# A hybrid three-branch layer on one core: one gate job fewer ahead of branch B, more gate work beside its units, and other block orders in branch A and in the output

## The chip, the cores and the metric

The kernel runs on one core of one Trainium2 chip. The metric is the device time of one launch in microseconds (us). A mark such as L648 is line 648 of the kernel before. The engines are PE (TensorE, matmuls and transposes), DVE (VectorE), ACT (ScalarE), POOL (GpSimd) and SP (SyncE, which here only issues DMAs; all loads and stores of this kernel go through its one queue, in order).

## What is computed

One layer on 2048 tokens of width 1024, in float32. After a layer norm, one wide projection (7592 columns) feeds three token mixers and their gates; in the reference's own words, cut:

```python
def _dsa_attention(q, k, v, iq, ik, iw):        # branch A, 8 heads, one key head
    ...
        _, idx = lax.top_k(score, n_sel)        # 256 keys of each query
    ...
        p = jax.nn.softmax(logits, axis=-1).astype(v.dtype)
        return jnp.einsum('bqhk,bqkd->bqhd', p, v_sel)

def _diff_attention(q, k, v, lam):              # branch B, 4 heads
    ...
        p = jax.nn.softmax(logits, axis=-1)
        a = (p[:, :, 0] - lam * p[:, :, 1]).astype(v.dtype)
        return jnp.einsum('bhqs,bshe->bqhe', a, v)

def _memory_attention(q, mk, mv):               # branch C, 4 heads, 256 memory tokens
    ...
```

Attention in A and B is chunk-causal: the block of queries number b (128 tokens, b = 0 to 15) sees (b + 1) * 128 keys, so block 15 is sixteen times as long as block 0. Each branch's output is multiplied by a SiLU gate ("sg"), projected to 1024 columns, weighted by a sigmoid gate ("tm"), summed, projected once more, added to the input and normalised.

## The kernel before, in words

Every float32 operand of a matmul is held as a high and a low part; `mm3` (L76 to L79) makes one product of three matmuls (high by high, high by low, low by high).

**Stages.** (1) The projections for A and B and A's top-k, whose result is a table of biases per block (`bias_d`, stored at L595). (2) The *gate jobs*: the list JOBS has 20 of them (2 "cq", 6 "sg", 12 "tm"), each for 256 columns and one half of the tokens. `gate_steps` does one job: a 2 MB load of weights `w` (L232), then 32 steps, each an `mm3` of 128x512 into PSUM tile `dps`; after each 8 steps a quarter of the job is finished by ACT and DVE and stored from tile `do` (L329, 256 KB, "sg_d" or "tm_d"). (3) Branch B. (4) Branch A. (5) Projections of B and C ("yps"), which need branch B and the gates only. (6) The projection of A for four pairs of blocks (`stage1`, tile `gT`), then per pair the last projection (tile `fz`) and the norm.

**Gate jobs of the first half of the tokens** are dealt out in three shares by `GB`: GB[0] jobs run as a block before branch B, the next GB[1] are handed out step by step within branch B, and the rest run after `run(fill)` (L915 to L918) together with the setup of the memory tokens (`do<-in_mem_dram`, L414, transposed by PE into `psT`, L183). The rest is written behind branch A, but the Tile framework's scheduler sets the order there and mixes it with branch A.

**Branch B** is a list of 64 units (4 heads, in each the blocks 15 down to 0). Inside `manual_schedule` the order of PE's instructions is that of the code. A unit has logits (tiles `lg` and `lgx`, L648 and L649, from keys `kg` and queries `bq`), a softmax on DVE and ACT, a mixture of two softmaxes on DVE (`mix`, L742, tile `P`), transposes (`pt`, L761) and products with the values (`ops`, L753). Logits run up to two units ahead. Between the parts, `pump(us)` hands out gate steps, counted at 0.69 us each:

```python
    for g in range(3, -1, -1):
        load_k(0, g)
        load_v(0, g)
    ...
    with tc.manual_schedule(engines={PE.engine}):
        pump(10.0)
        for _ in units[0].logits():
            pump(1.0)
    ...
            share = FILL[0] + FILL[1] * (u.b + 1)
    ...
                pump(share / m)
```

The loads of head 0 (`load_k` L679, `load_v` L685) and of the queries (`load_q`, L695) stand in SP's queue behind the last store of the top-k table, and SP issues in order. Keys and values of the next head are loaded as the tiles of the old one come free (after blocks 12, 8, 4 and 0). The output of a unit is stored at L791 (`ob_d`).

**Branch A** is `attn_a(b)`, called for b = 15 down to 0 (L912). Before the first block, keys `KA` (L848, 1 MB) and values `VA` (L850) are loaded into space that branch B leaves; each block loads its queries by eight DMAs (`aq`, L861) and its biases (L865). Per pair of heads there are logits with a running minimum on DVE, exponentials on ACT, transposes (`apt`), a split on ACT and DVE, and products (`aops`).

**Output order.** `PORD` is the order of the pairs of blocks in stage 6, and `LAST` the block whose final projection is cut into four pieces instead of two.

Of the kernel before, what the change touches and what calls it, by code (L numbers as in the profile page):

```python
# [22 lines left out]
NB = S // 128  # L23
NP = NB // 2
# [11 lines left out]
GV = 3  # L36
AHEAD = 1
EARLY = 4
PORD = list(range(NP - 1, -1, -1))
LAST = 2 * PORD[-1] + 1  # L40
WO = (1, 1)
YT = 8
YO = 1
APR = 2
GB = (4, 12)
FILL = (3.2, 0.08)
SQ_SCALE = 2.0 ** -80
SQ_LIM = 3.4028234663852886e38 * SQ_SCALE

# [9 lines left out]
def tile_layer(ctx, tc, x, mem, ln_in_g, ln_in_b, w_in, w_mem_kv, diff_lambda, diff_norm_g,  # L59
# [88 lines left out]
    def pool(name, bufs, space=None, side="left"):  # L148
        kw = {} if space is None else {"space": space}
        return tc.alloc_tile_pool(name=name, bufs=bufs, side=side, reuse_waits="tile", **kw)  # L150
# [59 lines left out]
    def reload(p):  # L210
        SP.dma_start(pair_of(p), ht_d[p])
# [182 lines left out]
    def gates(half, jobs, between=()):  # L394
        between = list(between)
        for i, (kind, c0, idx) in enumerate(jobs):
            yield from gate_steps(kind, half, c0, idx)
            if between:
                between.pop(0)()
        for f in between:  # L400
            f()

    def run(steps):
        for _ in steps:
            pass
# [11 lines left out]
    def dense_mem(j):  # L417
        w = dw.tile([128, 2, KT, 256], F32R, name="w")
        for i in range(2):
            for k in (4 * i, 4 * i + 2):  # L420
                raw = dw.tile([128, 2, 256], F32, name="wr", bufs=2)
                SP.dma_start(raw, w_view(w_mem_kv, k * 128, 2, 256 * j, 256))
                split(w[:, 0, k:k + 2], w[:, 1, k:k + 2], raw, G, G)
        ps = dqs.tile([128, 2, 256], F32, name="dps")
        for i in range(2):
            c = slice(i * 128, (i + 1) * 128)
            if j < 2:
                for k in range(KT):
                    mm3(ps[:, i], w[:, 0, k, c], w[:, 1, k, c], hm[0][:, 0, k], hm[0][:, 1, k], k == 0, k == KT - 1)
            else:  # L430
                for k in range(KT):
                    mm3(ps[:, i], hm[0][:, 0, k, c], hm[0][:, 1, k, c], w[:, 0, k], w[:, 1, k], k == 0, k == KT - 1)
        for i in range(2):
            o = dw.tile([128, 2, 256], F32R, name="do", bufs=3)
            if j < 2:
                split(o[:, 0], o[:, 1], ps[:, i], A, V)
                SP.dma_start(mk_d[:, 2 * j + i], o.bitcast(F32))
            else:
                h0 = 2 * (j - 2)
                ov = o.rearrange("p a (h d) -> p (a h d)", d=128).rearrange("p (h a d) -> p h a d", h=2, a=2)  # L440
                pv = ps[:, i].rearrange("p (h d) -> p h d", d=128)
                split(ov[:, :, 0], ov[:, :, 1], pv, A, V)
                SP.dma_start(mv_d[:, i, h0:h0 + 2].rearrange("p h a d -> p (h a d)"),
                             o.bitcast(F32).rearrange("p a c -> p (a c)"))
# [349 lines left out]
    for p in range(4):  # L794
        with tc.high_priority():
            reload(p)
    run(gates(0, JOBS[:GB[0]]))
    fill = gates(0, JOBS[GB[0]:GB[0] + GB[1]])
    owed = [0.0]

    def pump(us):
        owed[0] += us
        while owed[0] > 0:
            t = next(fill, None)
            if t is None:
                return
            owed[0] -= t
# [5 lines left out]
    with tc.manual_schedule(engines={PE.engine}):  # L813
        pump(10.0)
        for _ in units[0].logits():
            pump(1.0)
        units[0].mix()
        ahead = 1
        for i, u in enumerate(units):
            new = []  # L820
            while ahead < len(units) and ahead <= i + 2 and sum(x.slots for x in units[i:ahead + 1]) <= PB:
                new.append(units[ahead])
                ahead += 1
            share = FILL[0] + FILL[1] * (u.b + 1)
            m = 2 * (u.b // 4 + 1)
            n = sum(2 * (x.b // 4 + 1) for x in new)
            lg = (None for x in new for _ in x.logits())
            j = 0
            nxt = units[i + 1] if i + 1 < len(units) else None
            for t, _ in enumerate(u.values()):  # L830
                pump(share / m)
                while (j + 1) * m <= (t + 1) * n:
                    next(lg)
                    j += 1
                if t == m // 2 and nxt is not None and nxt not in new:
                    nxt.mix()
            for _ in lg:
                pass
            u.store()
            if nxt in new:  # L840
                nxt.mix()
# [67 lines left out]
            V.tensor_tensor(oo, oo, rc[:, 4 * h4:4 * h4 + 4, None].to_broadcast([128, 4, 64]), op=ALU.mult)  # L909
        SP.dma_start(oa_d[b], o.rearrange("p h d -> p (h d)"))  # L910

    for b in range(NB - 1, -1, -1):  # L912
        attn_a(b)

    run(fill)  # L915
    mp = pool("mp", 1)
    run(gates(0, JOBS[GB[0] + GB[1]:], [mem_setup] + [(lambda j=j: dense_mem(j)) for j in range(4)]))
    mp.release()  # L918
# [139 lines left out]
    def accs(ap, bufs):  # L1058
        return [ap.tile([128, 2, 256], F32, name="facc", bufs=bufs) for _ in range(4)]

    wo = []
    for i in range(EARLY):
        p = PORD[i]
        acc = accs(fs, 3)
# [20 lines left out]
    def ready(i):  # L1085
        if i >= NP:
            return
        p = PORD[i]
        acc = accs(fp, 4)
        if i < EARLY:  # L1090
            for u in range(4):
                SP.dma_start(acc[u], mg_d[p][:, 2 * u:2 * u + 2])
        else:
            stage1(p, acc)
        MT[p] = fp.tile([128, 2, KT, 256], F32R, name="fmT", bufs=AHEAD + 1)
        for u in range(4):
            H, L = (MT[p][:, a, 2 * u:2 * u + 2] for a in range(2))
            A.activation(H, acc[u], AF.Copy, scale=0.5)
            V.scalar_tensor_tensor(L, acc[u], 0.5, H.bitcast(F32), op0=ALU.mult, op1=ALU.subtract)

    def stage2(b):
        hh = fp.tile([128, D], F32, name="fh", bufs=3)
        SP.dma_start(hh, h_d[b])
        mT = MT[b // 2][:, :, :, 128 * (b % 2):128 * (b % 2) + 128]
        nz = 4 if b == LAST else 2
        for n in range(nz):
            c = slice(n * (D // nz), (n + 1) * (D // nz))
            z = fq.tile([128, 512], F32, name="fz")[:, :D // nz]
            for k in range(KT):
                mm3(z, mT[:, 0, k], mT[:, 1, k], wo[k][:, 0, c], wo[k][:, 1, c], k == 0, k == KT - 1)  # L1110
            V.scalar_tensor_tensor(hh[:, c], hh[:, c], ALPHA, z, op0=ALU.mult, op1=ALU.add)
        mu, rs = norm_stats(fp, hh, nz)
        if b != LAST:
            V.tensor_scalar(hh, hh, mu, rs, op0=ALU.subtract, op1=ALU.mult)
            G.tensor_tensor(hh, hh, gln, op=ALU.mult)
            V.tensor_tensor(hh, hh, bln, op=ALU.add)
            SP.dma_start(out[b * 128:(b + 1) * 128, :], hh)
            return
        for c in (slice(0, 512), slice(512, 1024)):
            V.scalar_tensor_tensor(hh[:, c], hh[:, c], mu, gln[:, c], op0=ALU.subtract, op1=ALU.mult)  # L1120
            V.scalar_tensor_tensor(hh[:, c], hh[:, c], rs, bln[:, c], op0=ALU.mult, op1=ALU.add)
            SP.dma_start(out[b * 128:(b + 1) * 128, c], hh[:, c])
# [3 lines left out]
    for p in range(NP):  # L1126
        ready(p + AHEAD)
        stage2(2 * PORD[p])
        stage2(2 * PORD[p] + 1)
    fq.release()  # L1130
# [54 lines left out]
```

## Time and profile before

| | us |
|---|---|
| three runs | 2928.38, 2924.34, 2923.38 |
| median | 2924.34 |
| profiled execution | 2925.13 |
| its span, first to last instruction | 2923.3 |
| PE busy in the span | 2778.1 (95%) |
| DVE, ACT, POOL busy | 2053.1, 1401.7, 864.6 |
| mean granted clock of PE | 0.982 |

The profiled execution has 1.8 us around its span. "Busy" is the time in which an engine has an instruction running; the clock is given as a share of 2.4 GHz, so that 0.50 is 1.2 GHz. The share of DMA is the mean busy share of the core's 16 DMA engines.

### The profile page before, as it was taken

To read this page: it belongs to the slowest core of one execution; us is meant where nothing else is said; L and a number is where in the kernel's file an instruction comes from. 1 tells how busy PE (TensorE), PEld (TensorE's weight loads), DVE (VectorE), ACT (ScalarE), POOL (GpSimd) and SP (SyncE) were. 2 spreads that over 40 slices of the span, in tenths; PEclk is the share of its full clock that TensorE was granted. 3 is DMA by queue.
4 is the path that set the end of the run, shared out by engine and by line. 5 is a ranking of instruction groups with operands and counts; after the bars stand their busy time and mean duration, and the time that the engine had idled before them with its cause. 6 is when DMAs were issued, how large, how long until landed. Compare 5 with 4: busy or idle time off the path is not lost.

```text
span 2923.3 us, 49093 instructions
## 1 busy us (share of the span) xinstructions
PE 2778.1 (95%) x17488; PEld 2490.2 (85%) x17488; DVE 2053.1 (70%) x4885; ACT 1401.7 (48%) x2716; POOL 864.6 (30%) x1270
## 2 busy tenths in 40 slices
PE   6899999999999989999999998998999999988998
PEld 6799989987788877788888887887999899987887
DVE  7179978898657887677777773447777777775554
ACT  3256755774346870344444442446555655552010
POOL 7454333235433302022222323121222222211322
PEclk9999999999999999999999999999999999998999
DMA  9666555564554576434334335235333333358542
GB/s 359 233 210 237 202 179 172 169 231 171 201 173 167 190 268 203 148 114 142 109 120 131 119 99 160 97 118 170 104 104 99 118 113 111 117 170 268 198 155 73
DMA packets 332020, 476.35 MB, mean 163 GB/s; under 512 B 28928, under 2 KB 252544, under 8 KB 323584
## 3 DMA queue, kind: packets, MB, share of 16 engines
q1 hardware_dynamic: 331776, 473.23, 49.5%
q8 instruction: 138, 2.26, 0.3%
q14 instruction: 106, 0.87, 0.1%
HBM read 271.25 MB, written 201.88 MB: 162 GB/s over the span
## 4 chain that ended last, share of the span: by engine, by line
PE 68%; DMA 7%; DVE 6%; issue 3%; POOL 2%; ACT 2%; SPq 1%; POOLq 0%; DVEq 0%; ACTq 0%
PE dps L77 9%; PE dps L78 9%; PE dps L79 9%; PE ops L753 4%; PE aops L898 4%; PE apt L893 3%; PE lg L648 3%; PE lg L649 3%; PE yps L77 2%; PE yps L78 2%; PE yps L79 2%; PE pt L761 2%; PE fz L77 2%; PE fz L78 2%; PE fz L79 2%
## 5 line engine op out<-in xcount | busy, mean ns | idle before, releaser
L77 PE MATMUL dps<-H,w 128*128 128x512 f32 x1280 | 518.5, 405 | 20.0 <-DVE do L328 5.7
L78 PE MATMUL dps<-H,w 128*128 128x512 f32 x1280 | 505.6, 395 | 0.0
L79 PE MATMUL dps<-H,w 128*128 128x512 f32 x1280 | 504.2, 394 | 0.0
L77 PE MATMUL dps<-w,H 128*128 128x256 f32 (+1 forms) x1152 | 342.1, 298 | 15.4 <-ACT w L71 8.6
L79 PE MATMUL dps<-w,H 128*128 128x256 f32 (+1 forms) x1152 | 339.8, 296 | 2.3 <-DVE H L74 2.3
L78 PE MATMUL dps<-w,H 128*128 128x256 f32 (+1 forms) x1152 | 340.7, 296 | 0.8 <-POOL w L74 0.8
L556 ACT ACTIVATE ja<-sall,thr 128x1280 bf16<-128x1280 f32 (+4 forms) x224 | 301.9, 1348 | 74.7 <-DVE thr L552 69.1
L543 DVE TENSOR_SCALAR_CACHE_REDUCE jd<-sall,thr 128x1408 bf16<-128x1408 f32 (+6 forms) x231 | 330.8, 1432 | 6.3
L77 PEld LDWEIGHTS dps<-H,w 128*128 128x128 f32 x1280 | 243.8, 190 | 64.8 <-issue 9.7
L79 PEld LDWEIGHTS dps<-H,w 128*128 128x128 f32 x1280 | 243.1, 190 | 51.2
L78 PEld LDWEIGHTS dps<-H,w 128*128 128x128 f32 x1280 | 243.8, 190 | 38.2
L651 DVE CUSTOM_DVE_ANT_0 AP<-lg,bias 128x512 f32<-128x512 f32 (+3 forms) x304 | 181.8, 619 | 124.7 <-PE lg L649 61.5
L516 DVE SCALAR_TENSOR_TENSOR sall<-ir,iw,sall 128x512 f32<-128x512 f32 (+3 forms) x266 | 191.9, 768 | 70.6 <-ACT ir L512 68.1
L77 PEld LDWEIGHTS dps<-w,H 128*128 128x128 f32 x1152 | 223.5, 194 | 18.1 <-ACT w L71 9.3
L71 ACT CAST apr<-apt 128x512 fp32r<-128x512 f32 (+1 forms) x288 | 157.5, 562 | 160.7 <-PE apt L893 129.5
L79 PEld LDWEIGHTS dps<-w,H 128*128 128x128 f32 x1152 | 223.1, 194 | 3.5 <-DVE H L74 2.7
L78 PEld LDWEIGHTS dps<-w,H 128*128 128x128 f32 x1152 | 223.5, 194 | 3.0 <-POOL w L74 2.2
L74 DVE TENSOR_TENSOR apr<-apt,apr 128x512 fp32r<-128x512 f32 (+1 forms) x288 | 185.5, 656 | 57.1 <-ACT apr L71 55.4
L898 PE MATMUL aops<-apr,VA 128*128 128x256 f32 x1088 | 209.0, 299 | 14.9 <-ACT apr L71 6.5
L69 POOL TENSOR_SCALAR w<-wr 128x512 fp32r<-128x512 f32 x120 | 87.1, 734 | 424.7 <-PE dps L79 339.2
L885 ACT ACTIVATE AP<-AP,anm 128x1024 f32<-128x1024 f32 (+7 forms) x192 | 172.1, 900 | 67.7 <-DVE anm L882 64.1
L512 ACT ACTIVATE ir<-ips 128x512 f32<-128x512 f32 (+3 forms) x304 | 150.0, 550 | 105.4 <-PE ips L507 92.0
(250 smaller groups left out, 6835.9 us busy)
## 6 DMA issues: line engine op xcount, KB each, us to landing
w_d<-w SPq DMA_DIRECT2D x28, 2048.0 KB, 7.3
w<-w_d SPq DMA_DIRECT2D x28, 2048.0 KB, 8.8
wr<-in_w_in_dram SPq DMA_DIRECT2D x108, 256.0 KB, 3.3
tm_d<-do SPq DMA_DIRECT2D x96, 256.0 KB, 2.9
bq<-qb_d SPq DMA_DIRECT2D x128, 128.0 KB, 3.3
aq<-qa_d SPq DMA_DIRECT2D x128, 128.0 KB, 3.1
yt<-tm_d SPq DMA_DIRECT2D x64, 256.0 KB, 3.5
sg_d<-do SPq DMA_DIRECT2D x48, 256.0 KB, 2.6
```

The costliest lines, as they stand in the source:

```text
L71: A.copy(H, src)
L74: el.tensor_tensor(L, src, H.bitcast(F32), op=ALU.subtract)
L77: PE.matmul(ps, lH, rH, start=start, stop=False)
L78: PE.matmul(ps, lH, rL, start=False, stop=False)
L79: PE.matmul(ps, lL, rH, start=False, stop=stop)
L512: A.activation(r[:, :cn], ps[:, :cn], AF.Relu)
L516: V.scalar_tensor_tensor(s[:, c0:c0 + cn], r[:, :cn], iw[:, h:h + 1], s[:, c0:c0 + cn], op0=ALU.mult, op1=ALU.add)
L543: V.tensor_scalar(jd[:, :L], sc[b], t.bitcast(F32)[:, i:i + 1], None, op0=op, op1=ALU.add, accum_out=dst[:, i:i + 1])
L556: A.activation(ja[:, :L], sc[b], AF.Sign, bias=thr.bitcast(F32)[:, i:i + 1], scale=-1.0, accum_out=cnt[:, i:i + 1])
L651: V.tensor_tensor_reduce(P[:, c0:c0 + cn], ps[:, :cn], bias[:, c0:c0 + cn], scale=-0.125, scalar=-LOW, op0=ALU.add, op1=ALU.min, accum_out ...
L885: A.activation(p[:, c0:c1], p[:, c0:c1], AF.Exp, bias=nm[:, e:e + 1], scale=-1.0, accum_out=sm[:, hd, i:i + 1])
L898: PE.matmul(o_ps.rearrange("p a d -> p (a d)"), VA[:, k0 + i], pr[:, a, i].rearrange("p e q -> p (e q)"), start=(k0 + i == 0 and a == 0), ...
```

## The change

Five edits, none of which changes what is computed or how many matmuls there are (17488 in both). The order of the output pairs becomes 0 to 7, and with it the block in four pieces becomes 15. One gate job fewer runs before branch B, and one more is handed out within it. The share of a unit goes from 3.2 + 0.08 (b + 1) to 3.7 + 0.065 (b + 1) us, and each chunk of the first logits is followed by 2.0 instead of 1.0 us of gate steps. Branch A's blocks run in another order.

```diff
-PORD = list(range(NP - 1, -1, -1))
+PORD = list(range(NP))
 LAST = 2 * PORD[-1] + 1
...
-GB = (4, 12)
-FILL = (3.2, 0.08)
+GB = (3, 13)
+FILL = (3.7, 0.065)
...
         pump(10.0)
         for _ in units[0].logits():
-            pump(1.0)
+            pump(2.0)
...
-    for b in range(NB - 1, -1, -1):
+    for b in [7, 0, 6, 1, 5, 2, 4, 3, 8, 9, 10, 11, 12, 13, 14, 15]:
         attn_a(b)
```

What this does to the order, at three places. The first is SP's queue at the end of the top-k and the start of branch B (`bias_d_128` is the last table of biases, `kg`, `vg`, `bq` are head 0's keys, values and queries, `sg_d` a finished quarter of a gate job). Before:

```order
L595 DMA bias_d_128<-pf 128x2048
L679 DMA kg<-kb_d_3_148 64x2x512 x2
L329 DMA sg_d_0_179<-do 128x512
L685 DMA vg<-vb_d_6_159 128x512
L685 DMA vg<-vb_d_7_160 128x512
...
L695 DMA bq<-qb_d_7_136 64x2x256 x2
L329 DMA sg_d_1_180<-do 128x512
L695 DMA bq<-qb_d_7_136 64x2x256 x2
```

Now:

```order
L595 DMA bias_d_128<-pf 128x2048
L679 DMA kg<-kb_d_3_148 64x2x512 x2
L685 DMA vg<-vb_d_6_159 128x512
L685 DMA vg<-vb_d_7_160 128x512
...
L695 DMA bq<-qb_d_7_136 64x2x256 x4
L695 DMA bq<-qb_d_6_135 64x2x256 x4
L329 DMA sg_d_0_179<-do 128x512
```

Up to the first pair of `kg` the queue is the same row for row (430 rows); then three stores of gate quarters that stood among the sixteen key and value loads and the first queries stand behind them. On PE, the first `lg` of branch B is row 6459 before and row 6363 now: 96 matmuls `dps` (32 steps) that stood ahead of it are gone from there, and nothing else ahead of it has moved. Behind it, 69 `dps` matmuls instead of 36 stand among the first unit's logits, 9 instead of 6 of them after its last.

The second place is SP's queue where the keys of head 3 begin to be loaded (`w` is the next gate job's 2 MB). Before:

```order
L791 DMA ob_d_219<-o 128x128
L329 DMA tm_d_1_196<-do 128x512
L791 DMA ob_d_218<-o 128x128
L679 DMA kg<-kb_d_0_149 64x2x512 x2
L695 DMA bq<-qb_d_6_143 64x2x256
...
L232 DMA w<-w_d_10527 128x4096
```

Now:

```order
L791 DMA ob_d_219<-o 128x128
L695 DMA bq<-qb_d_7_144 64x2x256
L791 DMA ob_d_218<-o 128x128
L232 DMA w<-w_d_10527 128x4096
L329 DMA tm_d_1_196<-do 128x512
L679 DMA kg<-kb_d_0_149 64x2x512 x2
```

The 2 MB load has moved from behind the keys to just ahead of them. The same meeting at the start of head 2 has `w` a few DMAs ahead of `kg` before and directly ahead of it now, and at the start of head 1 `w` has moved from ahead of `kg` to behind it.

The third is PE at the end of branch B and the start of branch A, from the last `ops` on (`psT` are transposes of the memory tokens). Before, 72 matmuls `dps` stand between the last `ops` and these rows:

```order
L648 MATMUL lg<-KA_19071,aq 128x512 x2
L649 MATMUL lg<-KA_19071,aq 128x512 x2
L183 MATMUL psT<-idf,do 128x128 x4
L648 MATMUL lg<-KA_19071,aq 128x512
L649 MATMUL lg<-KA_19071,aq 128x512
```

Now 14 matmuls `dps` stand between the last `ops` and these:

```order
L183 MATMUL psT<-idf,do 128x128 x12
L648 MATMUL lg<-KA_19071,aq 128x512 x2
L649 MATMUL lg<-KA_19071,aq 128x512 x2
L183 MATMUL psT<-idf,do 128x128 x4
L77 MATMUL dps<-H_257,w 128x512
```

58 matmuls have left the stretch in which PE waits for `KA` and the first `aq`, and three loads of memory tokens (`do`) and one of their weights now stand in SP's queue near the last `ob_d` store, ahead of `KA`. In all, 1216 instead of 1095 `dps` matmuls stand between branch B's first `pt` and its last `ops`. Further down, among the loads of the weights of stage 5, eight `aq` loads and one store of branch A now stand in SP's queue where there were none.

## Rows read from the trace of the kernel before

**Rows 1.** The page's busy times: engine, us, share, instructions.

```profile
PE 2778.1 (95%) x17488; PEld 2490.2 (85%) x17488; DVE 2053.1 (70%) x4885; ACT 1401.7 (48%) x2716; POOL 864.6 (30%) x1270
```

**Rows 2.** Windows from B's head to the end; columns in the first row.

```profile
core 0: us, PE busy (x) PEld busy (x) DVE busy (x) ACT busy (x) POOL busy (x), PEclk, DMA share, GB/s
1157.76:1181.10 23.34, 21.93 (x98) 17.86 (x96) 2.75 (x4) 2.39 (x4) 0.00 (x0) 1.00 1.03 278
1181.10:1201.06 19.96, 15.15 (x53) 11.79 (x53) 8.99 (x28) 5.39 (x6) 0.00 (x0) 0.83 0.46 163
1201.06:1788.26 587.20, 576.40 (x3350) 498.71 (x3350) 435.19 (x1521) 274.79 (x520) 159.69 (x441) 0.99 0.36 116
1788.26:1808.08 19.82, 16.74 (x76) 13.60 (x74) 0.59 (x3) 2.54 (x5) 5.41 (x11) 1.00 0.94 295
1808.08:1819.20 11.12, 6.55 (x28) 4.62 (x28) 4.59 (x14) 2.42 (x5) 3.68 (x5) 0.69 0.76 245
1819.20:1974.20 155.00, 153.17 (x934) 135.15 (x932) 70.28 (x182) 65.45 (x125) 23.22 (x25) 1.00 0.31 107
1974.20:2001.80 27.60, 20.70 (x118) 17.13 (x119) 23.77 (x51) 19.95 (x39) 1.36 (x2) 0.81 1.05 336
2001.80:2593.30 591.50, 574.11 (x4447) 542.85 (x4445) 439.31 (x1222) 346.12 (x813) 141.32 (x142) 1.00 0.36 107
2593.30:2629.40 36.10, 28.86 (x203) 26.56 (x203) 22.91 (x83) 15.05 (x48) 3.83 (x3) 0.91 0.69 215
2629.40:2668.50 39.10, 30.19 (x207) 28.61 (x207) 17.80 (x26) 9.40 (x16) 5.35 (x4) 0.83 0.93 306
2668.50:2923.30 254.80, 244.37 (x1338) 209.13 (x1336) 141.38 (x213) 28.93 (x48) 65.69 (x57) 0.99 0.47 153
```

**Rows 3.** A window in the gate jobs, PE alone; columns as above.

```profile
1139.62:1150.73 11.11, 11.11 (x50) 1.00 0.56 180
```

**Rows 4.** Timeline of PE at B's head: start, us, instruction, [idle before, releaser].

```profile
1157.76 0.39 PE L77 MATMUL dps<-H,w 128*128 128x512 f32 x1
...
1181.10 0.47 PE L648 MATMUL lg<-kg,bq 128*128 128x512 f32 x1 [1.41 <-DMA bq<-qb_d]
...
1182.68 0.77 PE L649 MATMUL lg<-kg,bq 128*128 128x512 f32 x1 [1.11 <-DMA bq<-qb_d]
...
1201.06 0.63 PE L761 MATMUL pt<-idf,P 128*128 128x128 f32 x4 [3.70 <-DVE P L742]
```

**Rows 5.** Timeline of SP's queue at B's head: start, us of issue, DMA.

```profile
1157.56 0.32 SPq L595 DMA_DIRECT2D bias_d<-pf  x1
1157.93 1.76 SPq L679 DMA_DIRECT2D kg<-kb_d  x2
1159.99 0.34 SPq L329 DMA_DIRECT2D sg_d<-do  x1
...
1174.83 0.33 SPq L329 DMA_DIRECT2D sg_d<-do  x1
1175.92 5.58 SPq L695 DMA_DIRECT2D bq<-qb_d  x6
```

**Rows 6.** Timeline of PE inside branch B: its waits at new heads.

```profile
1338.69 0.55 PE L648 MATMUL lgx<-kg,bq 128*128 128x512 f32 x1 [1.75 <-DMA kg<-kb_d]
...
1488.15 0.47 PE L648 MATMUL lg<-kg,bq 128*128 128x512 f32 x1 [3.17 <-DMA kg<-kb_d]
...
1503.21 0.47 PE L648 MATMUL lg<-kg,bq 128*128 128x512 f32 x1 [1.19 <-DVE mx L658]
...
1635.89 0.47 PE L648 MATMUL lg<-kg,bq 128*128 128x512 f32 x1 [1.92 <-DMA kg<-kb_d]
```

**Rows 7.** DMA issues: transfer, number, KB each, median us to landing.

```profile
w<-w_d SPq DMA_DIRECT2D x28, 2048.0 KB, 8.8
...
aq<-qa_d SPq DMA_DIRECT2D x128, 128.0 KB, 3.1
```

**Rows 8.** Timeline of SP's queue at the start of branch A.

```profile
1792.91 0.32 SPq L791 DMA_DIRECT2D ob_d<-o  x1
...
1795.21 0.42 SPq L848 DMA_DIRECT2D KA<-ka_d  x1
...
1796.14 5.08 SPq L861 DMA_DIRECT2D aq<-qa_d  x5
```

## The prediction

> **What bounds the kernel now.** I read the busy times first. PE is busy for 95% of the span [rows 1], no other engine for more than 70%, and the change leaves the number of matmuls as it is. So the time can only move by what PE loses: idle time, and time at a low granted clock. Second, I cut the span from branch B on into windows at the places where PE's work changes, and took as the loss of each its idle time plus (1 - clock) times its length [rows 2]. That gives, in order: B's head 1.4 and 8.2 us (windows 1 and 2), the body of B 16.7, the passage from B to A 3.1 and 8.0, A beside the last gate jobs 1.8, the passage to "yps" 12.1, yps beside A 17.4, the end of A 10.5, up to the first "fz" 15.6, the rest 13. Nothing ahead of 1157.76 us changes its order. Third, I looked in the timelines at what ends the waits inside these windows, and in the order at what now stands there.
>
> The sum is made against the profiled execution (2925.13 us, 0.8 above the median of 2924.34); the sum of differences is then added to the median.
>
> **B's head.** In the gate jobs PE does 49 steps of 128x512 from 1139.62 to 1150.73, 0.227 us each [rows 3]. The 96 matmuls that no longer stand ahead of the first logits are 21.8 us of work. It was exactly the work that covered the loads: the store of the last table of biases is issued at 1157.56, the first keys at 1157.93 [rows 5], and PE's first logits wait for the queries until 1181.10 and, for their second half, until 1182.68 [rows 4]. The table comes from DVE at the end of the top-k, which the change does not touch, and SP's queue holds keys, values and queries behind it. So PE will arrive at its first logits at 1157.76, where now the first of the 96 starts, and stand still until the queries land.
>
> When is that? Keys, values and the four query loads of the first unit are 4.72 MB (16 of 256 KB, 4 of 128 KB), the table is 0.52 MB. In the window in question the DMA engines are full (share 1.03) and move 278 GB/s [rows 2]. Three gate stores of 256 KB, the first and last of which are in [rows 5], no longer stand among them: 0.79 MB, 2.8 us at that rate. The second half of the first logits thus starts at 1182.68 - 2.8 = 1179.9, and PE is idle for 22.1 us where it was for 2.5 (1.41 + 1.11). The wait for the mixture on DVE, 3.70 us [rows 4], shrinks by the three matmuls that now stand behind the last logits, 0.7 us. Sum: 22.1 - 2.5 - 0.7 = **+18.9**. From below, I take the densest stretch of the trace, 336 GB/s [rows 2]: 5.24 MB need 15.6 us, which leaves 15.6 - 2.5 - 0.7 = +12.4. From above, without any gain from the stores: 24.9 - 2.5 = +22.4. I stay near the upper part because the 278 GB/s are of these very transfers, and the 336 are of others.
>
> The Trainium skill speaks against so long a wait: "DMA: Bandwidth & Descriptors", section "Specifications", gives about 358 GB/s as what one core gets from HBM, by which 5.24 MB would take 14.6 us and this term would be +11.4. The trace does not agree here: it shows full engines at 278 GB/s. The rule has its place among the rivals.
>
> What happens to the 21.8 us? They are not lost: the steps are now handed out within B, so that they leave the end of the program shorter, but only if they fall into holes of PE, or push other work into holes. Otherwise PE's work is the same, and the idle time is added in full.
>
> **The body of B.** 121 more matmuls stand between first pt and last ops, 27.4 us at 0.227. They make units longer and so help against waits on DVE: three waits for "mx" of 1.19 us each (one of them stands in [rows 6]). What else is idle there is the wait for the keys of a new head, 1.75, 3.17 and 1.92 us; with 3.6 for mx that is 10.4 of the 10.8 idle us of the window [rows 2, 6]. Unit times don't touch the landing of the keys as such: they are loaded when a tile of the old head comes free. But the weights of a gate job, 2 MB that take 8.8 us [rows 7], have moved against them in the queue: at the first new head to behind the keys (-1.75), at the second to directly ahead, at the third from behind to ahead. Each of the latter two costs between 0 and 8.8 us; I take half, 4.4 each, since logits run two units ahead. Waits for mx and the low clock behind a wait give back about 3. Sum: -1.75 + 8.8 - 3 = **+4**, with -16.7 (the whole loss of the window) and +12 as the ends.
>
> **From B to A.** The outputs of the last unit are stored 4.65 us after the last ops (1788.26 to 1792.91), KA is issued 2.3 us later and the first logits of A come 12.87 us after that (1795.21 to 1808.08) [rows 2, 8]. The distance is set by transfers and stays at about 19 us, but of PE's 72 gate matmuls in it 14 are left (3.2 us), and 12 short transposes (1.3 us). The handed-out work has run out too early: 4 x (16 x 3.7 + 0.065 x 136) + 10 + 16 = 298 us are asked for, 13 jobs of 32 steps at 0.69 are 287. Idle time there is about 15 instead of 3.1 us; of the work taken away 17 matmuls (3.9 us) now stand in the stretch behind, which lost 8.0. Sum: 11.8 - 3.8 = **+8**, from +2 (the tm_d store ahead of KA goes faster, and the stretch behind fills) to +13.
>
> **A beside the last gate jobs.** Short blocks have more waits per matmul than block 15, but gate work lies beside them: **+1** (0 to +3).
>
> **The passage to yps.** Here the engines are full with the weights of B's and C's projections (share 1.05 at 336 GB/s [rows 2]), and eight aq loads and a 256 KB store of A now stand among them: 1.3 MB, 3.9 us: **+4** (0 to +8).
>
> **yps beside A.** Blocks 8 to 15 now run here and at the end, in which DVE and ACT have long pieces of work; the loss of 17.4 should fall a little: **-4** (-12 to +6).
>
> **The end of A.** Before, the last blocks are the shortest, with hardly any matmuls to hide a softmax, and 10.5 us are lost. Now block 15 is last, with long runs of transposes and products: **-9** (-10.5 to -4).
>
> **Up to the first fz.** The stage waits for weights and gate tiles whatever the pair's number: **-2** (-5 to +3). The output order itself is free: all pairs cost the same, and the last block is cut in four either way. 0.
>
> Sum: 18.9 + 4 + 8 + 1 + 4 - 4 - 9 - 2 = +20.9, so 2925.13 becomes 2946.0 and the median 2924.34 becomes **2945 us**.
>
> **The rivals.** A measurement of this kernel tells 0.2% (5.8 us) from no change.
>
> *The holes in B close.* If the added gate work covers all of B's waits, the body gives back 16.7 instead of costing 4: 20.9 - 20.7 = +0.2, 2924.5 us, no change. For it: the holes are waits of 1 to 3 us, and a unit gets 0.3 to 0.5 us more gate work. Against: three of them wait for keys that SP issues late, and two got a 2 MB load ahead. 0.14.
>
> *The end closes* (the other side). What is lost from 2001.80 to 2668.50 is 17.4 + 10.5 + 15.6 = 43.5 us. If long blocks at the end of A run beside the loads and products of stage 5 and 6 so that nothing is lost there, the first terms (+31.9) and the passage (+4) stand against -43.5: -7.6, 2917 us. It decides from 36 us given back on, and counts as faster from 42. For it: no short block is left where gate work is gone. Against: 15.6 of it wait for loads after A. 0.08.
>
> *The loads are quicker alone.* At 336 GB/s the head costs 12.4 instead of 18.9: 2938.5 us. Against it, the full engines at 278. 0.08. By the 358 GB/s of the Trainium skill ("DMA: Bandwidth & Descriptors", section "Specifications") the estimate would be 2937.5 us.
>
> *SP's queue jams under short blocks.* Each block issues eight aq loads, five in 5.08 us [rows 8], so 8.1 us per block. Blocks 0 and 1 have less work than that; two blocks waited out in full add 16 us: 2961 us. Against it: gate jobs lie beside them. 0.10.
>
> **How the numbers follow.** The forecast has 0.60. The terms' ends, taken as independent (the root of the sum of squares), reach 25 us below and 17 above 2945, of which I take nine tenths below, so the range is 2922 to 2963. It takes in the first rival and the last two. Faster by over 0.2% is the second alone, 0.08; within 0.2% the first, 0.14; slower the rest, 0.78.
>
> **What would show it.** In the changed profile PE stands idle from 1157.8 to about 1180 with the queries' DMA as releaser, and DMA share near 1. The waits of 3.17 and 1.92 for kg grow, that of 1.75 goes. Between last ops and first lg of A some 15 us are idle. No wait for amx of several us is left at A's end. The forecast is wrong in kind if PE does not wait 20 us at B's head, or if the stretch from 2001.80 on gives back more than 30 us.

## The result and the profile after

The changed kernel takes 2952.05 us (median of four runs, 2949.79 to 2956.82), the kernel before beside it 2925.2: the ratio is 1.0108, with a 95% interval of 1.0088 to 1.0128. It is slower, by 27 us (the medians). The profiled execution took 2949.79 us, with a span of 2948.0, against 2925.13 and 2923.3. The mean granted clock is 0.978 instead of 0.982, PE is busy for 2775.9 us.

The same windows as in [rows 2], cut at the same events, on the changed kernel (window, us, busy time of each engine with its count, PEclk, DMA share, GB/s; the seventh and eighth end at the first "yps" and the last):

```profile
1160.70:1178.34 17.64, 0.17 (x1) 0.03 (x1) 0.00 (x0) 0.00 (x0) 0.00 (x0) 0.64 1.05 278
1178.34:1203.16 24.82, 21.60 (x86) 17.08 (x86) 9.69 (x29) 5.99 (x7) 0.00 (x0) 0.91 0.41 136
1203.16:1826.60 623.44, 605.18 (x3472) 522.91 (x3472) 442.27 (x1524) 278.50 (x526) 160.81 (x441) 0.98 0.36 115
1826.60:1843.19 16.59, 5.66 (x29) 4.22 (x28) 2.67 (x6) 2.51 (x5) 7.93 (x13) 0.74 0.78 247
1843.19:1855.11 11.92, 9.23 (x29) 6.65 (x30) 3.11 (x9) 1.71 (x3) 1.89 (x2) 0.65 0.60 153
1855.11:1981.72 126.61, 126.61 (x781) 113.23 (x780) 50.63 (x166) 49.29 (x108) 22.69 (x24) 1.00 0.38 125
1981.72:2024.07 42.35, 31.30 (x176) 24.88 (x174) 33.83 (x107) 28.40 (x67) 1.45 (x2) 0.88 1.02 302
2024.07:2620.27 596.20, 584.44 (x4507) 552.43 (x4506) 456.66 (x1234) 356.21 (x825) 141.22 (x142) 1.00 0.35 105
2620.27:2651.32 31.05, 27.70 (x225) 26.46 (x224) 18.11 (x32) 11.73 (x21) 3.81 (x3) 1.00 0.58 171
2651.32:2690.91 39.59, 28.84 (x211) 26.98 (x210) 16.51 (x26) 8.56 (x15) 5.20 (x4) 0.87 0.89 304
2690.91:2948.00 257.09, 243.20 (x1335) 209.27 (x1333) 140.81 (x214) 29.68 (x49) 62.32 (x57) 0.99 0.47 152
```

The first row is the new hole: PE is idle for 17.5 us at branch B's head, with full DMA engines (share 1.05) at 278 GB/s, where [rows 2] have 21.93 us of work. In the timeline of PE (start, us, instruction, idle before and releaser), against [rows 4]:

```profile
1160.48 0.39 PE L79 MATMUL dps<-H,w 128*128 128x512 f32 x1
1178.34 0.77 PE L648 MATMUL lg<-kg,bq 128*128 128x512 f32 x1 [17.47 <-DMA bq<-qb_d]
1179.39 0.77 PE L649 MATMUL lg<-kg,bq 128*128 128x512 f32 x1 [0.28 <-DMA bq<-qb_d]
1179.95 0.63 PE L77 MATMUL dps<-H,w 128*128 128x512 f32 x1
```

PE comes to its first logits 2.9 us later than 1157.76, though the order ahead of it is the same; the queries land at the time that the prediction gave, to 0.5 us, but by two errors that cancel: the loads were issued 1.3 us later and took 1.8 us less than it had said. SP's queue there, against [rows 5], has no gate store between the loads and the queries any more:

```profile
1158.88 0.32 SPq L595 DMA_DIRECT2D bias_d<-pf  x1
1159.25 1.36 SPq L679 DMA_DIRECT2D kg<-kb_d  x2
...
1170.85 7.07 SPq L695 DMA_DIRECT2D bq<-qb_d  x8
1182.82 0.33 SPq L329 DMA_DIRECT2D sg_d<-do  x1
```

Inside branch B, the waits for the keys of new heads, against [rows 6]:

```profile
1346.33 0.47 PE L648 MATMUL lgx<-kg,bq 128*128 128x512 f32 x1 [1.07 <-DMA kg<-kb_d]
...
1504.35 0.76 PE L648 MATMUL lg<-kg,bq 128*128 128x512 f32 x1 [7.50 <-DMA kg<-kb_d]
...
1662.21 0.77 PE L648 MATMUL lg<-kg,bq 128*128 128x512 f32 x1 [4.20 <-DMA kg<-kb_d]
```

1.75, 3.17 and 1.92 us have become 1.07, 7.50 and 4.20. At the second of them SP's queue shows the 2 MB of a gate job just ahead of the keys:

```profile
1493.06 0.32 SPq L232 DMA_DIRECT2D w<-w_d  x1
1493.47 0.58 SPq L679 DMA_DIRECT2D kg<-kb_d  x1
1494.15 0.57 SPq L329 DMA_DIRECT2D tm_d<-do  x1
1494.77 0.58 SPq L679 DMA_DIRECT2D kg<-kb_d  x1
```

Inside branch B the waits for "mx", the minima that DVE takes of a unit's logits, which were 3.6 us before, are still there:

```profile
PE lg L648 <- DVE mx L658: 3.0, 2, 1.9
PE lgx L648 <- DVE mx L658: 1.8, 1, 1.8
```

(Instruction, who was waited for: us in total, times, longest.)

**Where the 24.7 us went.** The table below takes for each stretch its time less its matmuls at their pace (0.227 us for 512 columns, 0.12 for 256; the counts are those of the order), and shows the difference to the kernel before, in the profiled executions. The stretches end at B's first "pt", B's last "ops", A's first "apt", the last "dps", the first "yps", the last "yps", the first "fz", the last "fz". The columns e1 to e12 are the experiments further down. In five kernels whose order is the same up to A (before, e3, e5, e11, e12) the first row differs by up to 7 us and the second by 3, so smaller differences say nothing. Each column is a single execution: that of e8 is 7 us faster than e8's median, that of e12 5 us.

| us against before | after | e1 | e2 | e3 | e4 | e5 | e6 | e7 | e8 | e9 | e10 | e11 | e12 |
|---|---|---|---|---|---|---|---|---|---|---|---|---|---|
| up to B's first pt | +16.3 | +16.8 | +0.4 | +1.6 | +6.7 | -1.6 | -1.3 | +17.2 | -4.2 | -2.4 | -6.2 | -3.8 | -5.7 |
| body of B | +8.6 | +4.2 | +18.0 | -0.6 | +8.9 | -3.2 | +20.8 | -1.3 | -3.3 | +6.6 | -1.2 | -1.0 | -1.3 |
| B to A | +7.9 | -10.7 | -0.7 | -2.7 | +7.7 | -1.9 | -0.7 | -10.7 | -10.7 | +9.0 | -1.8 | +0.2 | -5.5 |
| A beside gate jobs | -2.2 | +0.4 | -2.7 | -0.3 | -2.2 | -1.0 | -3.5 | +2.6 | +0.6 | +0.9 | -0.7 | 0.0 | +12.4 |
| up to yps | +6.7 | +1.1 | +9.0 | +6.1 | +10.6 | +8.2 | +2.6 | +2.9 | +4.0 | +9.0 | +8.6 | -0.1 | +4.6 |
| yps beside A | -7.2 | -9.6 | -13.6 | -7.2 | -7.1 | -6.4 | -3.0 | +6.9 | -2.9 | +0.4 | -6.1 | -0.7 | -0.6 |
| up to the first fz | -7.9 | -3.5 | -2.0 | +13.4 | -5.6 | -13.0 | +3.4 | +3.1 | -6.4 | -12.0 | -12.1 | +18.5 | -4.8 |
| fz | +2.5 | -1.9 | -6.9 | +0.1 | -1.4 | -0.6 | -6.6 | +1.0 | +0.2 | -0.2 | +0.7 | -0.2 | -0.5 |

### The profile page after: what moved, and what is told of

It is laid out like the page before. It is cut to its first block, busy times and chain, and to the rows that moved or that the text cites. A ratio compares the mean times of both kernels' runs of the same rounds, so it can differ in the third digit from the quotient of the medians.

```text
span 2948.0 us, 49101 instructions
## 1 busy us (share of the span) xinstructions
PE 2775.9 (94%) x17488; PEld 2489.7 (84%) x17488; DVE 2059.1 (70%) x4885; ACT 1401.7 (48%) x2716; POOL 859.8 (29%) x1270
## 4 chain that ended last, share of the span: by engine, by line
PE 67%; DMA 8%; DVE 6%; issue 3%; ACT 2%; POOL 2%; SPq 0%; POOLq 0%; DVEq 0%; ACTq 0%
PE dps L77 10%; PE dps L78 10%; PE dps L79 10%; PE ops L753 4%; PE aops L898 3%; PE lg L648 3%; PE lg L649 3%; PE apt L893 3%; PE pt L761 2%; PE yps L77 2%; PE yps L78 2%; PE yps L79 2%; PE fz L79 2%; PE fz L78 2%; PE fz L77 2%
## 5 line engine op out<-in xcount | busy, mean ns | idle before, releaser
L77 PE MATMUL dps<-H,w 128*128 128x512 f32 x1280 | 520.7, 407 | 18.9 <-DVE do L328 5.9
```

Source lines behind the costliest of these rows:

```text
L77: PE.matmul(ps, lH, rH, start=start, stop=False)
```

## The experiments

All were timed beside the kernel before, on one chip per group of four; the medians of before were 2920.7, 2922.5 and 2922.0 us. Theory: the loss is the sum of what the stretches lose, above all B's head, where 96 matmuls no longer cover the loads. Rivals: branch A's order carries the loss; or the moved work fills other holes.

**e1: one gate job fewer ahead of B, alone.**

```diff
-GB = (4, 12)
+GB = (3, 13)
```

> The kernel before with one edit alone: GB = (3, 13). Theory (the loads of branch B's head need the 96 matmuls ahead of the first logits as cover): 13 to 17 us slower than before at the head, PE idle there 15 to 18 us, and since only one of the jobs moves, nothing of it comes back; in all 2938 to 2945 us. Rival 1 (the loss lies in branch A's block order and its loads): within 4 us of before. Rival 2 (the 96 matmuls come back as filling of other holes): within 4 us of before, although the idle time at the head is there.

2918.68 us, ratio 1.0000 (0.9990 to 1.0011): no change. The total is what rival 2 said, and the theory's is wrong. But the hole is there, 18.77 us, with full DMA engines at 292 GB/s (the first line is the window up to the first logits, the second is of PE's timeline):

```profile
1158.47:1177.39 18.92, 0.15 (x1) 0.03 (x1) 0.00 (x0) 0.00 (x0) 0.00 (x0) 0.61 1.05 292
1177.39 0.77 PE L648 MATMUL lg<-kg,bq 128*128 128x512 f32 x1 [18.77 <-DMA bq<-qb_d]
```

It comes back further on. The old FILL asks for 266 us in branch B, and thirteen jobs give 287, so that some 21 us of gate steps are left at B's end. They fill the passage to A entirely, which lost 11 us before. The two windows from the last "ops" to A's first "apt", against the fourth and fifth window of [rows 2]:

```profile
1782.19:1802.96 20.77, 20.77 (x94) 17.21 (x93) 0.59 (x3) 2.54 (x5) 2.89 (x8) 1.00 0.99 311
1802.96:1816.80 13.84, 13.84 (x63) 11.40 (x61) 4.14 (x13) 3.46 (x6) 0.00 (x0) 1.00 0.62 226
```

Busy for every one of 34.6 us, at full clock. A further 9.6 us less are lost beside A, under the same block order; why was not settled.

**e2: the change with the old GB.**

```diff
-GB = (3, 13)
+GB = (4, 12)
```

> The changed kernel with GB put back to (4, 12). Theory: the head is as before (PE idle under 4 us), 13 to 17 us come back; the gate steps handed out in branch B run out earlier (298 us asked, 265 there), so the passage from B to A stays as costly as in the change: 2932 to 2940 us. Rival 1 (branch A's order): 2945 or more. Rival 2: as the change, 2950, since the holes in B are no longer filled.

2927.01 us, 1.0022 (1.0011 to 1.0033): 25 us less than the change, more than expected. The head's hole is gone (waits of 1.29 and 1.25 us); but the body of B costs 18 us, and the gain beside and after A is larger than in the change. The passage to A, which was expected to cost as much as in the change, costs no more than before (-0.7).

**e3: branch A's order alone.**

```diff
-    for b in range(NB - 1, -1, -1):
+    for b in [7, 0, 6, 1, 5, 2, 4, 3, 8, 9, 10, 11, 12, 13, 14, 15]:
```

> The kernel before with branch A's new block order alone. Theory: the passage to the projections of B and C costs 4 to 8 us more, the stretch beside A and A's end give back 10 to 15: 2916 to 2926 us. Rival 1 (the loss of the change lies in this order): 2935 or more.

2934.26 us, 1.0050 (1.0033 to 1.0066): slower, against the theory. The stretch up to the first "fz" loses 13 us more. PE's waits there (engine, instruction, who was waited for: us in total, times, longest):

```profile
PE gT L77 <- ACT yoT L945: 12.0, 3, 6.9
PE gT L942 <- DMA fo<-oa_d: 5.9, 1, 5.9
```

Before, in the same stretch:

```profile
PE lg L648 <- DVE amx L658: 4.5, 1, 4.5
PE gT L77 <- ACT yoT L945: 1.8, 2, 1.5
PE gT L942 <- DMA fo<-oa_d: 0.3, 1, 0.3
```

The old output order begins with pair 7, blocks 15 and 14, which this order of A computes last. Stage 6 now waits for A's last outputs: in SP's queue its loads stand directly behind A's last store.

```profile
2614.97 0.32 SPq L910 DMA_DIRECT2D oa_d<-ao  x1
2616.99 0.80 SPq L1049 DMA_DIRECT2D fo<-oa_d  x2
```

**e4: queries first at B's head, in the change.**

```diff
+    load_q(0, NP - 1)
     for g in range(3, -1, -1):
         load_k(0, g)
+    for g in range(3, -1, -1):
         load_v(0, g)
```

> The changed kernel with one edit: at branch B's head the four query loads of the first unit are issued first, then the four key tiles, then the values (0.5 + 2.1 MB instead of 4.7 MB have to land for the first unit's logits). Theory: PE's idle time at the head falls from 17.5 to between 4 and 9 us, and the time by 8 to 12, to 2940 to 2944 us. Rival 2 (the idle time at the head is not on the path, or is only moved to the wait for the mixture): less than 3 us gained.

2943.58 us, 1.0081 (1.0063 to 1.0099): 8.5 us less than the change by the medians, 8 by the ratios, whose intervals just overlap. PE stands for 7.84 us instead of 17.47:

```profile
1169.47 0.77 PE L648 MATMUL lg<-kg,bq 128*128 128x512 f32 x1 [7.84 <-DMA kg<-kb_d]
```

The rest of the program loses what it lost in the change, within the noise of the table. The hole at the head is on the path there.

**e5: both orders, without the edits in branch B.**

```diff
-PORD = list(range(NP - 1, -1, -1))
+PORD = list(range(NP))
...
-    for b in range(NB - 1, -1, -1):
+    for b in [7, 0, 6, 1, 5, 2, 4, 3, 8, 9, 10, 11, 12, 13, 14, 15]:
```

> The kernel before with branch A's new order and the new output order, nothing else. Theory: the new output order begins with pairs that branch A finished long ago, so the wait for A's last outputs that the block order alone brought (13 us up to the first fz) turns into the 8 us gain that the change showed there: 2908 to 2920 us. Rival (branch A's order costs 10 us by itself): 2930 or more.

2906.96 us, 0.9954 (0.9937 to 0.9970): faster by 13 us (the ratio), at the far end of what was expected. Up to the first "fz" 13 us less are lost, instead of 13 more in e3; the 4.5 us wait for "amx" at A's end, shown under e3 for the kernel before, is not there any more. The two lines of e3 here:

```profile
PE gT L77 <- ACT yoT L945: 5.5, 2, 4.7
PE gT L942 <- DMA fo<-oa_d: 2.2, 2, 2.0
```

**e6: the new FILL and the 2.0 us alone.**

```diff
-FILL = (3.2, 0.08)
+FILL = (3.7, 0.065)
...
-            pump(1.0)
+            pump(2.0)
```

> The kernel before with the new FILL and the 2.0 us beside the first logits, nothing else. Theory (handing out more than there is costs in branch B, because the steps cover nothing in the early units and are missing in the last): B's body loses 14 to 20 us more than before, the passage to A about the same as before: 2930 to 2942 us. Rival (the new FILL is harmless; the head and branch A carry the loss): 2916 to 2926.

2936.56 us, 1.0055 (1.0037 to 1.0073): slower, as expected. B's body loses 20.8 us more. Among its waits the keys grow to 11.9 us from 5.1, and new ones appear at L779, in the last units, where the steps have run out (no gate matmul stands in B's last 19 us, 1805.7 to 1824.9):

```profile
PE lg L648 <- DMA kg<-kb_d: 11.9, 2, 7.6
PE ops L753 <- DVE o L779: 8.1, 3, 4.4
```

**e7: the change with the old FILL and 1.0 us.**

```diff
-FILL = (3.7, 0.065)
+FILL = (3.2, 0.08)
...
-            pump(2.0)
+            pump(1.0)
```

> The changed kernel with the old FILL and the old 1.0 us beside the first logits. Theory: PE is still idle 18 us at B's head, but the job moved into branch B is not used up there, and its rest fills the passage from B to A, whose loss of 18.6 us falls under 2: 2915 to 2930 us. Rival (idle time at B's head is lost for good, whatever lies behind): 2937 or more.

2949.4 us, 1.0107 (1.0088 to 1.0126): a miss. The passage from B to A went to nothing, as expected (from +7.9 to -10.7 in the table), and the body of B by 10 us; and nearly all of it is lost again from the first "yps" on, 14 us beside A (-7.2 to +6.9) and 11 up to the first "fz". A's last product starts 12 us before the last "yps" (2606.73 and 2618.59), and then nothing covers the step to stage 6:

```profile
2618.59 0.28 PE L79 MATMUL yps<-yoT,H 128*128 128x256 f32 x1
2631.68 1.11 PE L942 MATMUL gT<-idf,fo 128*128 128x128 f32 x4 [12.81 <-DMA fo<-oa_d]
```

In SP's queue, that load stands behind the store of the last pair of stage 5:

```profile
2623.85 0.32 SPq L1035 DMA_DIRECT2D mg_d<-yt  x1
2627.80 0.32 SPq L1049 DMA_DIRECT2D fo<-oa_d  x1
```

In the change, A still has products up to 2651, 31 us behind its last "yps" at 2620, and covers it. That 13 us are lost at this seam is shown; why the scheduler's mixture uses A up sooner here is not, and where the 14 us beside A go was not followed either.

**e8: four jobs ahead, thirteen within, the old FILL, both orders, and queries first.**

```diff
-GB = (3, 13)
-FILL = (3.7, 0.065)
+GB = (4, 13)
+FILL = (3.2, 0.08)
...
-            pump(2.0)
+            pump(1.0)
```

(against the changed kernel; with e4's edit as well)

> GB = (4, 13): the four jobs ahead of branch B as before, thirteen handed out in it; the old FILL and 1.0; branch A's and the output's new order; and the first unit's queries loaded first, then keys, then values. Theory: no idle time at B's head (gain of 2 to 5 against before), leftover gate steps fill the passage from B to A (gain 8 to 11), the end as in the change (gain 8 to 12 after the dearer passage to the projections): 2897 to 2910 us. Rival (stretches don't add; one gain is given back elsewhere): 2915 or more.

2909.79 us, 0.9961 (0.9948 to 0.9973): faster than before, at the upper end of what was expected. The passage gains 11 us, as in e1; the 4 us of the head are less than what equal orders differ by. The medians tell no gain over e5, although e8's profiled execution, the fastest of its twelve, has a span of 2900.7 us against 2903.7. From A on, e5 loses 12.8 us less than before, e8 only 4.5. The rival, that the stretches don't simply add, holds in part.

**e9: the change with four jobs ahead of B.**

```diff
-GB = (3, 13)
+GB = (4, 13)
```

> The changed kernel with GB = (4, 13): four jobs ahead of branch B again, thirteen handed out in it, three instead of four left beside branch A. Theory (the change's loss at the head is the one missing job ahead of it): the head's idle time falls from 17.5 to under 4 us, the body of B and the passage to A stay as in the change: 2930 to 2942 us. Rival (the job ahead is worth nothing, or what it gains is lost beside A, where a job is now missing): 2945 or more.

2940.6 us, 1.0057 (1.0040 to 1.0074): 11.5 us less than the change. The first row of the table goes from +16.3 to -2.4, body and passage stay at +6.6 and +9.0, and PE waits for the queries for 1.5 us instead of 17.5. In this pair of kernels the head's hole costs most of its length.

**e10: both orders and queries first.**

```diff
-PORD = list(range(NP - 1, -1, -1))
+PORD = list(range(NP))
...
-    for b in range(NB - 1, -1, -1):
+    for b in [7, 0, 6, 1, 5, 2, 4, 3, 8, 9, 10, 11, 12, 13, 14, 15]:
```

(with e4's edit as well)

> The kernel before with the new order of branch A, the new output order, and the first unit's queries loaded first. Theory: the 2907 us of the two orders, less 3 to 6 us at B's head: 2899 to 2906 us. Rival (head time is absorbed behind): 2907 or more.

2905.8 us, 0.9945 (0.9928 to 0.9963): the fastest of all, though not told from e5 and e8, whose intervals overlap with it. What queries first are worth with four jobs ahead stays under the noise.

**e11: the output order alone.**

```diff
-PORD = list(range(NP - 1, -1, -1))
+PORD = list(range(NP))
```

> The kernel before with the new output order alone. Prediction's term for it: 0, 2916 to 2926 us. Theory now (an output order that begins with the pairs that branch A finishes last waits for them): 6 to 14 us slower, 2928 to 2938 us, all of it between the last yps and the first fz.

2940.98 us, 1.0065 (1.0046 to 1.0084): slower by 19 us, a little more than expected, and all of it up to the first "fz" (+18.5). With A from 15 down, pair 0 is the last that A finishes, and the waits are those of e3:

```profile
PE gT L77 <- ACT yoT L945: 12.3, 3, 7.2
PE gT L942 <- DMA fo<-oa_d: 5.9, 1, 5.9
```

**e12: blocks 0 to 15 in plain order, with the new output order.**

```diff
-    for b in range(NB - 1, -1, -1):
+    for b in range(NB):
```

> The kernel before with branch A's blocks in the plain order 0 to 15 and the new output order. Theory (what counts is that the long blocks come last and that the output begins with blocks finished long ago; how 0 to 7 are mixed counts little): within 8 us of the 2907 of the mixed order. Rival (the mixing of short and middle blocks is what gains): 2918 or more.

2928.73 us, 1.0019 (1.0005 to 1.0033): the theory is wrong here, and the rival right: the mixing of short with middle blocks matters. A beside the gate jobs loses 12.4 us more, and the gain up to the first "fz" is 4.8 us instead of e5's 13.0. Beside the gate jobs it is small waits, the first of them for the gate jobs' own weights:

```profile
PE dps L77 <- DMA w<-w_d: 4.4, 2, 2.4
PE aops L898 <- DVE apr L74: 2.6, 3, 1.3
PE apt L893 <- ACT AP L885: 2.5, 2, 2.0
```

## Why the prediction was right, point by point

The sign, the size (2945 against 2952) and the main place were right. That the terms add up to +20.9 where the table has +24.7 is in part luck: the head was put 5.5 us too high, the body of B 4.6 too low. By its steps:

- **B's head**, +18.9: in mechanism right, in size too high. The first row of the table has +16.3, of which 2.9 are PE's later arrival, which is not the change's: 13.4. The wait itself came to 17.75 us (17.47 and 0.28) instead of 22.1, in three parts: the second half of the first logits started 20.1 us after the first keys were issued, not 22 (1159.25 to 1179.39); PE had come 2.9 us later to loads that were issued 1.3 us later; and the 22.1 counted the first half's own matmul, 0.8 us, as idle time. The stretch to the first "pt" lost another 1.2 us less, to the low clock (2.2 us against 3.4); its wait for the mixture shrank from 3.70 to 2.9, as said. By the words of its own sign ("if PE does not wait 20 us") the forecast would be wrong in kind; but the wait is where it was said to be, and e4 and e9 show it to be on the path, so the sign was set too tight.
- **The rate of these loads.** It was the right one: 278 GB/s with full engines, in the very window (e1 shows 292 in the same place). With it the cause of the rival of quicker loads is refuted, though its price, +12.4, is nearer to the 13.4 than the forecast's. The 336 GB/s that bound the term from below are not the densest stretch of the trace, as the prediction says; a window further on has 387 (last section). The Trainium skill ("DMA: Bandwidth & Descriptors", section "Specifications") gives about 358 GB/s as a core's limit from HBM. As a price for these transfers the trace disagrees with it, with its 278; as a limit it is passed in the window with 387.
- **The body of B**, +4: +8.6. The key waits went as argued, down at the first head (by 0.7, not to nothing) and up by 4.3 and 2.3 at the others, +5.9 in all. What failed is the 3 us that the added work was to give back: the waits for "mx" went from 3.6 to 4.8 us, and the 121 matmuls gave back nothing. e6 shows it more plainly.
- **From B to A**, +8: +7.9, right in place, the size partly by luck. PE was idle for 10.9 us between the last "ops" and A's first logits, not 15, since these came 9.5 us after `KA` was issued (1833.72 to 1843.19), not 12.87; the stretch behind gave back less than was said. The step that the handed-out work runs out is too simple. What the passage loses goes with the gate matmuls that stand in it, from the last "ops" to A's first "apt": 72 before; 31 in the change, e4 and e9, which lose 8 to 9 us more; 140, 119 and 119 in e1, e7 and e8, where thirteen jobs met the old FILL and the passage lost nothing. In e2 and e6 the steps run out earlier still, but the scheduler has drawn on jobs that are written further behind, 56 and 77 matmuls stand there, and the passage loses as before.
- **A beside the gate jobs and the passage to yps**, +1 and +4: -2.2 and +6.7, together as said.
- **yps beside A**, -4: -7.2. **A's end and up to the first fz**, -9 and -2: -7.9 together; no wait for "amx" of several us is left at A's end, as said.
- **The output order**, 0: this step failed. It is not free: alone it costs 19 us (e11), because "all pairs cost the same" leaves out when A finishes each. Nor is A's order a gain by itself (e3). What the prediction put down to long blocks at A's end is shown to need both: the two together gain 13 us (e5). In the change both were made, so that the sum did not show the error.
- **The rivals.** That the holes in B close was wrong: in no kernel with the new FILL did the body lose less. That the end closes was right in sign, but by 15 us between the first "yps" and the first "fz" (two rows of the table), not 36. SP's queue under short blocks: 8 "aq" in 8.03 us were issued at A's start, but no stretch shows the 16 us.

What the prediction did not see is how far edits depend on each other. Without the orders, one job fewer ahead of B costs nothing (e1); with them and the old FILL it costs 42 us (the medians of e7 and e5). The sum over stretches of one given kernel held; a sum over edits would not: e1, e5 and e6 add up to about +3 us, and the change measured +27.

## What to carry to other kernels

Work that stands ahead of a long wait is cover, and its price is read from the end of what it covers (here loads that SP issues only behind the top-k's last store), not from its own length; loading first what the first consumer needs took over half of that wait here (17.47 to 7.84 us, e4), the job put back ahead of it nearly all (1.5 us, e9). Count what a filler is asked for against what it has: steps handed out early to units that need none are missing in the last units and at the next passage, and steps left over fill it. An order of producing and an order of consuming are one edit: judge them together, since each alone can lose what both gain.

## What the runs showed of the hardware

With the DMA engines full (share 1.05), the loads of keys, values and queries move 278 to 292 GB/s, while the weights of the projections reach 336 at the same share [rows 2], and a stretch of the kernel before, ahead of the first "fz", 387 (PE alone; clock, DMA share, GB/s at the end):

```profile
2649.70:2659.90 10.20, 6.86 (x29) 0.50 1.06 387
```

Full engines do not tell the rate. The low clock cost no more behind the longer wait: after 17.5 us of idle time PE's first matmuls of 512 columns are shown with 0.63 us each instead of 0.39, and the window up to the first "pt" has a granted clock of 0.91, 2.2 us of its 24.82; before, after waits of 1.41 and 1.11 us, the same window had 0.83, 3.4 us of 19.96 [rows 2, 4]. In the changed kernel the clock had already fallen while PE was idle: from 1166 to 1178 us it stands at 0.50, which is 1.2 GHz.
